# Score matmuls of a two-layer trunk: the keys' low parts in tiles of their own, zero on the other rows

## The chip, the cores and the metric

The kernel runs on one core of one Trainium2 chip. The metric is the device time of one execution in microseconds (us), the median over the runs; smaller is better. The engines are named as the profile names them: PE is TensorE's matmul, PEld its load of the stationary operand, DVE is VectorE, ACT is ScalarE, POOL is GpSimd, SP is SyncE, which here only issues DMAs.

## The reference

A trunk of two layers works on 256 latent tokens and 256 context tokens of width 1024. Each layer is a half-step SwiGLU FFN, a token mixer and a second half-step FFN, each behind an RMS norm that is modulated by a conditioning vector. Layer 0 mixes with differential attention (8 heads, two softmax maps of 64 features each), layer 1 with grouped-query attention (16 query heads, 4 key heads of 64 features, queries and keys normalised). Latent tokens attend to all 512 keys, context tokens to the 256 of the context.

```python
def _diff_attend(q, k, v, lam):
    s = jnp.einsum("bqhmd,bkhmd->bhmqk", q, k).astype(jnp.float32) * DA_HEAD_DIM ** -0.5
    p = jax.nn.softmax(s, axis=-1)
    p = (p[:, :, 0] - lam * p[:, :, 1]).astype(v.dtype)
    return jnp.einsum("bhqk,bkhe->bqhe", p, v)
...
def gqa_attend(q, k, v, scale):
    s = jnp.einsum("bqhgd,bkhd->bhgqk", q, k).astype(jnp.float32) * scale
    p = jax.nn.softmax(s, axis=-1).astype(v.dtype)
    return jnp.einsum("bhgqk,bkhd->bqhgd", p, v)
```

## The kernel before

Everything is held feature-major: 128 features on the partitions, tokens along the free dimension. An fp32 operand is split exactly into two float32r parts, hi and lo, and a product is the sum of three matmuls (`mac`, L383): hi with hi, hi with lo, lo with hi. Weights come in 512 KB pieces through SP's DMA queue, ACT makes the hi part (L152) and DVE the lo part (L153).

Scores need only 64 features, half of the 128 rows. So the kernel stacks the parts. `stack_q` (L606) puts the hi part of a map's or head's queries on its own 64 rows and the lo part on the other 64. `stack_k` (L616) puts the hi part of the keys on both halves. One matmul over all 128 rows (L626) then gives hi·hi and lo·hi together. The third term, the queries' hi part with the keys' lo part, is a second matmul over the 64 own rows alone (L627). Both maps of a head (m = 0, 1) share one tile `kl` for the lo parts: map 0 on rows 0 to 63, map 1 on rows 64 to 127. In the grouped-query layer two key heads share a `kl` in the same way.

Differential attention runs 8 heads of 4 units, a unit being 128 queries; units 0 and 1 (latent) see 512 keys, units 2 and 3 (context) 256. Each unit has two maps, so two pairs of score matmuls. After the scores come a DVE reduction (L733), the exponential on ACT (L734), DVE's normalisation and difference of the maps (L738 to L740), and one unit later PE's transposes (L750) and, once a head, the outputs (L761). Between the units stand products of the next head (`qk_proj`, `v_proj`) or of the output projection. The grouped-query layer runs 32 units of one pair each, 512 keys wide: reduction L1007, exponential L1009, normalisation L1011, transposes L1017 (up to two units later), outputs L1027 on 64 columns of the array, with query projections and pieces of the output projection between some units.

The order of instructions on each engine is set by the tile framework's scheduler, from the program's order and its own costs; the engines run their lists in order and wait on semaphores. Tiles are buffers of a pool; a tag with `bufs=n` has n of them, and a new tile waits until the old one's last reader is done.

At the head of differential attention, `lambdas` (L680) makes the scalar lambda from four vectors, `lamv`, that `late_constants` (L88) had loaded on SP's queue, and the context's norm is worked in among the first products: its sums of squares (`ms`, L272), 1/rms on ACT and DVE (L283 to L288, last `rsq`), its spread over the partitions on PE (`bc`, L315), and eight normalised tiles, each in a temporary `ht` (tag "ht", three buffers), as hi (L344) and lo (L345). The rotary embedding (`rotate`, L596) has one multiplication on POOL (L603). `sck` holds the conditioning vectors for the first norm's shift and scale. `pT` are the transposed weights of a unit (L751).

Of the kernel before, what the change touches and what calls it, by code (L numbers as in the profile page):

```python
# [19 lines left out]
P = 128  # L20
# [28 lines left out]
def trunk(ctx: ExitStack, tc: tile.TileContext, a: dict):  # L49
# [17 lines left out]
    tok = (slice(0, SEQ), slice(SEQ, T))  # L67
    sck = const.tile([P, KD, 32], F32, name="sck")
# [16 lines left out]
    lamv = const.tile([P, 4, 64], F32, name="lamv")  # L85
    rope = const.tile([P, 2, SEQ], F32, name="rope")

    def late_constants():  # L88
        nc.sync.dma_start(final_g, a["final_g"])
        nc.sync.dma_start(subln_g, a["da_subln_g"])  # L90
        nc.sync.dma_start(qk_g[:, 0:1], a["gqa_q_norm_g"])
        nc.sync.dma_start(qk_g[:, 1:2], a["gqa_k_norm_g"])
        for i, n in enumerate(("da_lam_q1", "da_lam_k1", "da_lam_q2", "da_lam_k2")):
            nc.sync.dma_start(lamv[:, i, :], a[n].to_broadcast([P, 64]))
        nc.sync.dma_start(rope, a["rope"])
# [17 lines left out]
    # a chunk is (its source, k tiles of each piece, columns of a k tile)  # L113
# [85 lines left out]
    def mod_first(pool, j):  # L199
        """Shift and scale of the first norm's feature tile j, on the tensor engine."""  # L200
# [26 lines left out]
    def first_rstd(pool, fp):  # L227
        """1 / rms of each token of both streams, on every partition."""
        ms = ax_tile("ms0")
        for j in range(0, KD, 2):  # L230
            sq = [fp.tile([P, T], F32, tag=t, name=f"sq_{t}") for t in ("sg", "av")]
            for i in range(2):
                nc.scalar.activation(sq[i], x[j + i], AF.Square)
            nc.vector.tensor_tensor(sq[0], sq[0], sq[1], op=ALU.add)
            for t in range(4):
                # one group for the whole bank
                nc.tensor.matmul(
                    ms[:, t : t + 1], sq[0][:, t * P : t * P + P], ones_d, start=(j, t) == (0, 0),
                    stop=(j, t) == (KD - 2, 3),
                )  # L240
# [12 lines left out]
    acc = [[stat.tile([P, 256], F32, name=f"sqacc{s}", tag=f"sqacc{s}"), None] for s in range(2)]  # L253

    def sq_add(j, s):
        if j == 0:
            nc.scalar.activation(acc[s][0], x[j][:, tok[s]], AF.Square)
        elif j == KD - 1:
            # the last feature tile's stay apart: the tensor engine adds them
# [7 lines left out]
    def mean_squares(s):  # L267
        ms = ax_tile("ms")
        for i in range(2):
            for t in range(2):  # L270
                # one group for the bank
# [6 lines left out]
    def rsqrt(pool, ms, n, scale=1.0, eng=nc.vector, tag="rsq"):  # L278
        """1 / sqrt(scale * ms + EPS), [P, n]: from the table's, made exact by a Newton step."""
# [11 lines left out]
    def rsqrt_free(pool, ms, n, scale=1.0, tag="rsq"):  # L291
        """1 / sqrt(scale * ms + EPS), [P, n], of positive values and without a table: from the halved
        exponent's bits, then a cubic and a Newton step."""
# [17 lines left out]
    def spread(r):  # L311
        """r, by tokens, on every partition."""
# [9 lines left out]
    def rms_rstd(s):  # L322
        """1 / rms of each token of a stream, on every partition."""
        return spread(rsqrt(tmp, mean_squares(s)[:, 0:2], 2))

    def table(func, after):
        """Has the activation table of func loaded once `after` is there."""
# [21 lines left out]
    def gained_shift(l, n3, j):  # L349
        """The shift as two more tokens, in parts."""  # L350
# [3 lines left out]
    def gained_tile(l, n3, j):  # L354
        """x times the norm's gain, without 1 / rms, which is a factor of each token."""
# [6 lines left out]
    # the context's norm, in steps that the next sublayer's first products are set between  # L362
# [20 lines left out]
    def mac(out, lhs, rhs, first, last):  # L383
        """out += lhs.T @ rhs, from the parts (hi, lo) of both."""
# [31 lines left out]
    def gained(j):  # L416
        """x times the final gain, by tokens."""
# [15 lines left out]
    def boundary(groups, nxt, follow):  # L433
        """The last products of a sublayer, first for the latent tokens, whose next norm then runs
        under the products for the context. A group is (outs, ends, tiles)."""
# [15 lines left out]
    def ffn(l, s, n, follow=None, f_steps=0, o_steps=0, upto=(0, 0)):  # L451
# [5 lines left out]
        with ExitStack() as st:  # L457
# [22 lines left out]
            def gated_late(i, gate, up):  # L480
                """Of products without 1 / rms, with those of the shift behind them."""
# [114 lines left out]
    def rotate(pool, t, tiles=1):  # L596
        """Axial rotary of t, [P, tiles * SEQ], in place."""
# [8 lines left out]
    def stack_q(q, st, scale):  # L606
        """Parts of -scale * the queries of two maps or heads (rows 0-63 and 64-127), each as one
        stack of hi and lo; hi stays on its own rows. scale is a power of two, or its negative."""
# [6 lines left out]

    def stack_k(k, st, lo):  # L616
        """Parts of the keys of two maps or heads: hi on both halves of the rows, lo on its own."""
        for m in range(2):
# [3 lines left out]
            nc.vector.tensor_tensor(lo[own], k[own], st[m][own].bitcast(F32), op=ALU.subtract)  # L622

    def scores(ps, q, k, k_lo, m):
        """ps = queries.T @ keys from the stacks of one map or head."""
        nc.tensor.matmul(ps, q, k, start=True, stop=False)  # L626
        nc.tensor.matmul(ps, q[HALF[m]], k_lo[HALF[m]], start=False, stop=True)  # L627
# [8 lines left out]
    def out_proj(base, parts, part, l, n, half, follow=None):  # L636
        """x += gate * (half of the heads) @ w_o; parts of these heads' outputs."""
# [34 lines left out]
    def diff_attention(l):  # L672
        base = start["att", l]
        scale = 64 ** -0.5
        with tc.tile_pool(name="da", bufs=2) as ap:
            lam = ap.tile([P, 4], F32, tag="lam", name="lam", bufs=1)
            nlam = lam[:, 3:4]
            g1 = ap.tile([P, 1], F32, tag="g1", name="g1", bufs=1)

# [22 lines left out]
            def stacks(qps, kps):  # L702
# [8 lines left out]
                kl = ap.tile([P, T], F32R, tag="kl", name="kl")  # L711
# [4 lines left out]
            # A unit is 128 queries of a head: of latent tokens (u = 0, 1) with all keys, of context  # L716
            # tokens (u = 2, 3) with the context's.
# [4 lines left out]
            def weights_of(hd, u):  # L722
                """Both maps' softmax and their difference."""
# [6 lines left out]
                for m in range(2):  # L730
                    sps = ax_tile("sps")
                    scores(sps[:, :nk], qs[m][:, tq], ks[m][:, k0:], kl[:, k0:], m)
# [12 lines left out]
            def turned(hd, u):  # L745
# [5 lines left out]
                pT = ap.tile([P, 4, P], F32, tag="pT", name="pT", bufs=4)  # L751
                nc.scalar.activation(pT[:, : nk // P, :].rearrange("p k q -> p (k q)"), tps[:, :nk], AF.Copy)
# [20 lines left out]
            def normed(hd):  # L773
                """1 / rms of the outputs of a pair of heads."""
# [10 lines left out]
            def parts_of(hd, hi, lo):  # L785
                """Feature-major, with the gain, in parts."""
# [11 lines left out]
            def behind(hd, u):  # L798
                """What follows a unit's weights, once the next unit's are under way."""
# [33 lines left out]
            def qk_proj(h, g):  # L833
# [4 lines left out]
                if g:  # L838
                    sts[h] = stacks(qks[h, 0], ps)
# [4 lines left out]
            def fillers(h):  # L844
                """Products between the units of head h, by unit."""
                if h == HEADS - 1:
                    # the norms' outputs are not needed from here on
# [26 lines left out]
            sts[0] = stacks(*qkps)  # L874
# [25 lines left out]
    def gqa(l):  # L900
        base = start["att", l]
        scale = 64 ** -0.5
        with tc.tile_pool(name="gq", bufs=2) as ap:
            qs = [ap.tile([P, SEQ], F32R, tag=f"qs{i % 8}", name=f"qs{i}", bufs=1) for i in range(16)]
            ks = [ap.tile([P, T], F32R, tag=f"ks{i}", name=f"ks{i}", bufs=1) for i in range(4)]
            kl = [ap.tile([P, T], F32R, tag=f"kl{i}", name=f"kl{i}", bufs=1) for i in range(2)]
# [8 lines left out]
            def rms_of(sq, tag, rsqrt):  # L915
                """1 / rms over the 64 features of each token of [P, 512]: by tokens, [P, 4 x 2 heads]."""
# [28 lines left out]
            def q_out(i, ps):  # L945
                sq = squares(ps)
                # the norm itself, a factor of each query, waits for the exponent
# [39 lines left out]
            for g in range(2):  # L987
                kn = k_normed(kps[g], kr[g])
                stack_k(kn, ks[2 * g : 2 * g + 2], kl[g])
# [5 lines left out]
            # A unit is 128 queries (qi) of one head (hb) of a tile t.  # L995
            def weights_of(t, qi, hb):
# [4 lines left out]
                scores(sps, qs[2 * t + hb][:, qi * P : qi * P + P], ks[2 * g + hb], kl[g], hb)  # L1001
# [180 lines left out]
```

## Time and profile before

| | |
|---|---|
| time, median of 3 runs | 1755.96 us (1752.56 to 1759.06) |
| profiled execution, first to last instruction (span; the profile leaves no other time of it) | 1750.3 us |
| PE busy | 1736.8 us, 99% of the span |
| PEld busy | 1469.2 us, 84% |
| DVE busy | 1162.5 us, 66% |
| ACT busy | 733.5 us, 42% |
| POOL busy | 22.1 us, 1% |
| granted TensorE clock, mean | 0.995 |
| differential attention's units | about 437 to 632 us of the span |
| grouped-query units | about 1448 to 1534 us of the span |

Matmuls are pipelined: a record's duration runs into those after it, so that the time that a matmul takes of the engine is read from its start to the next one's start, or from the chain of waits, which gives each piece the time that it adds. A PE that is busy is not PE at its peak. "issue" as the end of a wait means that the profile shows nothing that was waited for. Times below are from the span's start.

### The profile page before, as it was taken

To read this page: it belongs to the slowest core of one execution; us is meant where nothing else is said; L and a number is where in the kernel's file an instruction comes from. 1 tells how busy PE (TensorE), PEld (TensorE's weight loads), DVE (VectorE), ACT (ScalarE), POOL (GpSimd) and SP (SyncE) were. 2 spreads that over 40 slices of the span, in tenths; PEclk is the share of its full clock that TensorE was granted. 3 is DMA by queue.
4 is the path that set the end of the run, shared out by engine and by line. 5 is a ranking of instruction groups with operands and counts; after the bars stand their busy time and mean duration, and the time that the engine had idled before them with its cause. 6 is when DMAs were issued, how large, how long until landed. Compare 5 with 4: busy or idle time off the path is not lost.

```text
span 1750.3 us, 24875 instructions
## 1 busy us (share of the span) xinstructions
PE 1736.8 (99%) x9586; PEld 1469.2 (84%) x9586; DVE 1162.5 (66%) x2113; ACT 733.5 (42%) x1359; POOL 22.1 (1%) x34
## 2 busy tenths in 40 slices
PE   9999999999999999999999999999999999999998
PEld 6788888889778789888888898888888897699998
DVE  3697786757777778765866557545452498776664
ACT  3432222235656656222222244322232377765454
POOL 0000000000000000000000000000000000000000
PEclk8999999999999999999999999999999999999999
DMA  7675655442112122545644535446552331145652
GB/s 258 226 237 166 191 204 185 151 138 87 59 49 73 60 86 85 200 135 158 203 151 165 155 111 190 151 125 197 177 162 79 109 121 49 49 151 154 215 155 87
DMA packets 76870, 249.58 MB, mean 143 GB/s; under 512 B 9937, under 2 KB 10065, under 8 KB 76753
## 3 DMA queue, kind: packets, MB, share of 16 engines
q1 hardware_dynamic: 76032, 247.38, 43.7%
q8 instruction: 75, 1.23, 0.3%
q10 hardware_dynamic: 720, 0.62, 0.1%
q14 instruction: 43, 0.34, 0.1%
HBM read 246.92 MB, written 1.05 MB: 142 GB/s over the span
## 4 chain that ended last, share of the span: by engine, by line
PE 98%; DVE 1%; ACT 0%; issue 0%; POOL 0%; DVEq 0%; ACTq 0%
PE out L387 7%; PE out L388 7%; PE out L386 7%; PE gate L386 7%; PE gate L388 7%; PE up L388 7%; PE gate L387 7%; PE up L386 7%; PE up L387 7%; PE sps L627 2%; PE qk L386 2%; PE g L386 2%; PE qk L388 2%; PE qk L387 2%; PE sps L626 2%; PE g L387 2%
## 5 line engine op out<-in xcount | busy, mean ns | idle before, releaser
L152 ACT ACTIVATE whi<-raw 128x1024 fp32r<-128x1024 f32 (+3 forms) x426 | 350.9, 836 | 485.3 <-PE out L387 253.2
L153 DVE TENSOR_TENSOR wlo<-raw,whi 128x1024 fp32r<-128x1024 f32 (+3 forms) x426 | 399.6, 946 | 194.5 <-ACT whi L152 193.8
L174 DVE CUSTOM_DVE_ANT_0 junk<-wm,sc,b_mod 128x1024 bf16<-128x1024 f32 x224 | 287.4, 1283 | 179.0 <-DMA wm<-in_w_mod 175.1
L386 PE MATMUL gate<-hhi,whi 128*128 128x512 f32 (+1 forms) x648 | 233.8, 361 | 0.0
L388 PE MATMUL gate<-hhi,wlo 128*128 128x512 f32 (+1 forms) x648 | 233.8, 361 | 0.0
L387 PE MATMUL up<-hlo,whi 128*128 128x512 f32 (+1 forms) x648 | 233.7, 361 | 0.0
L387 PE MATMUL gate<-hlo,whi 128*128 128x512 f32 (+1 forms) x648 | 233.7, 361 | 0.0
L386 PE MATMUL up<-hhi,whi 128*128 128x512 f32 (+1 forms) x648 | 233.7, 361 | 0.0
L388 PE MATMUL up<-hhi,wlo 128*128 128x512 f32 (+1 forms) x648 | 233.7, 361 | 0.0
L387 PE MATMUL out<-alo,whi 128*128 128x512 f32 (+1 forms) x638 | 232.6, 365 | 0.0
L388 PE MATMUL out<-ahi,wlo 128*128 128x512 f32 (+1 forms) x638 | 232.2, 364 | 0.0
L386 PE MATMUL out<-ahi,whi 128*128 128x512 f32 (+1 forms) x638 | 232.1, 364 | 0.0
L387 PEld LDWEIGHTS out<-alo,whi 128*128 128x128 f32 x638 | 119.9, 188 | 21.5 <-DVE alo L405 0.4
L386 PEld LDWEIGHTS gate<-hhi,whi 128*128 128x128 f32 x648 | 122.3, 189 | 18.5 <-ACT sg L474 0.2
L387 PEld LDWEIGHTS up<-hlo,whi 128*128 128x128 f32 x648 | 122.3, 189 | 18.4
L388 PEld LDWEIGHTS gate<-hhi,wlo 128*128 128x128 f32 x648 | 122.3, 189 | 18.4
L388 PEld LDWEIGHTS up<-hhi,wlo 128*128 128x128 f32 x648 | 122.3, 189 | 18.3
L386 PEld LDWEIGHTS up<-hhi,whi 128*128 128x128 f32 x648 | 122.3, 189 | 18.3
L387 PEld LDWEIGHTS gate<-hlo,whi 128*128 128x128 f32 x648 | 122.3, 189 | 18.3
L386 PEld LDWEIGHTS out<-ahi,whi 128*128 128x128 f32 x638 | 120.0, 188 | 20.9
L388 PEld LDWEIGHTS out<-ahi,wlo 128*128 128x128 f32 x638 | 119.9, 188 | 21.0
L404 ACT ACTIVATE ahi<-av 128x512 fp32r<-128x512 f32 (+1 forms) x88 | 50.8, 578 | 181.3 <-DVE av L476 174.1
(239 smaller groups left out, 2630.8 us busy)
## 6 DMA issues: line engine op xcount, KB each, us to landing
raw<-in_w_in SPq DMA_DIRECT2D x170, 512.0 KB, 4.5
wm<-in_w_mod SPq DMA_DIRECT2D x128, 512.0 KB, 4.2
raw<-in_w_out SPq DMA_DIRECT2D x64, 384.0 KB, 3.2
raw<-in_w_out SPq DMA_DIRECT2D x64, 320.0 KB, 3.1
raw<-in_da_vqk SPq DMA_DIRECT2D x24, 512.0 KB, 3.6
wf<-in_w_mod SPq DMA_DIRECT2D x16, 512.0 KB, 4.7
raw<-in_gq_qkv SPq DMA_DIRECT2D x12, 512.0 KB, 3.7
raw<-in_da_o SPq DMA_DIRECT2D x8, 512.0 KB, 3.6
```

Source lines behind the costliest of these rows:

```text
L152: nc.scalar.activation(hi[:, c], raw[:, c], AF.Copy)
L153: nc.vector.tensor_tensor(lo[:, c], raw[:, c], hi[:, c].bitcast(F32), op=ALU.subtract)
L174: nc.vector.tensor_tensor_reduce(out=junk, in0=raw, in1=mod_pool["sc"][:, s, :], op0=ALU.mult, op1=ALU.add, scale=1.0, scalar=b_mod[:, l, ...
L386: nc.tensor.matmul(out, ah, bh, start=first, stop=False)
L387: nc.tensor.matmul(out, ah, bl, start=False, stop=False)
L388: return nc.tensor.matmul(out, al, bh, start=False, stop=last)
L404: nc.scalar.activation(hi, src, AF.Copy)
L626: nc.tensor.matmul(ps, q, k, start=True, stop=False)
L627: nc.tensor.matmul(ps, q[HALF[m]], k_lo[HALF[m]], start=False, stop=True)
```

## The change

Each map or key head gets a `kl` tile of its own, [128, 512]; the lo part stays on its own 64 rows, and the other 64 rows are set to zero once, by POOL, at the start of each attention (`zero_others`, 8 memsets in all). The second score matmul then goes over all 128 rows with the same stationary queries as the first: the zero rows add nothing. In differential attention the four `kl` tiles are made once (two per head, taken in turn by even and odd heads).

The added tiles take space, and four tiles move for it. `lamv` is loaded by ACT's DMA queue at the start of differential attention into an `ht` buffer, no longer by SP among the late constants; `sck` lies in a temporary; `pT` has two buffers of 512 and two of 256 columns, before four of 512.

```diff
+    sck = tmp.tile([P, KD, 32], F32, tag="sq", name="sck")
...
-        for i, n in enumerate(("da_lam_q1", "da_lam_k1", "da_lam_q2", "da_lam_k2")):
-            nc.sync.dma_start(lamv[:, i, :], a[n].to_broadcast([P, 64]))
...
+    def zero_others(lo):
+
+        for m in range(2):
+            nc.gpsimd.memset(lo[m][HALF[1 - m]].bitcast(F32), 0.0)
...
-            nc.vector.tensor_tensor(lo[own], k[own], st[m][own].bitcast(F32), op=ALU.subtract)
+            nc.vector.tensor_tensor(lo[m][own], k[own], st[m][own].bitcast(F32), op=ALU.subtract)
...
-        nc.tensor.matmul(ps, q[HALF[m]], k_lo[HALF[m]], start=False, stop=True)
+        nc.tensor.matmul(ps, q, k_lo, start=False, stop=True)
...
+            lamv = tmp.tile([P, 4, 64], F32, tag="ht", name="lamv")
+            for i, n in enumerate(("da_lam_q1", "da_lam_k1", "da_lam_q2", "da_lam_k2")):
+                nc.scalar.dma_start(lamv[:, i, :], a[n].to_broadcast([P, 64]))
+
+            kls = [[ap.tile([P, T], F32R, tag=f"kl{i}{m}", name=f"kl{i}{m}", bufs=1) for m in range(2)] for i in range(2)]
+            for kl in kls:
+                zero_others(kl)
...
-                kl = ap.tile([P, T], F32R, tag="kl", name="kl")
+                kl = kls[h % 2]
...
-                    scores(sps[:, :nk], qs[m][:, tq], ks[m][:, k0:], kl[:, k0:], m)
+                    scores(sps[:, :nk], qs[m][:, tq], ks[m][:, k0:], kl[m][:, k0:])
...
-                pT = ap.tile([P, 4, P], F32, tag="pT", name="pT", bufs=4)
+                pT = ap.tile([P, nk // P, P], F32, tag=f"pT{nk}", name="pT")
...
-            kl = [ap.tile([P, T], F32R, tag=f"kl{i}", name=f"kl{i}", bufs=1) for i in range(2)]
+            kl = [ap.tile([P, T], F32R, tag=f"kl{i}", name=f"kl{i}", bufs=1) for i in range(4)]
+            for g in range(2):
+                zero_others(kl[2 * g : 2 * g + 2])
...
-                scores(sps, qs[2 * t + hb][:, qi * P : qi * P + P], ks[2 * g + hb], kl[g], hb)
+                scores(sps, qs[2 * t + hb][:, qi * P : qi * P + P], ks[2 * g + hb], kl[2 * g + hb])
```

On PE one thing moves. At the head of differential attention the spread of the context's 1/rms (`bc`) stands, before, right behind the last product for the values (`v`) and ahead of the first for queries and keys (`qk`):

```order
L388 MATMUL v_3281<-whi_1_3236,hlo_141 128x256
L315 MATMUL bc<-ident,rsq 128x128 x2
L386 MATMUL qk_3282<-hhi_126,whi_0_3251 128x256
L387 MATMUL qk_3282<-hlo_134,whi_0_3251 128x256
L388 MATMUL qk_3282<-hhi_126,wlo_0_3252 128x256
```

Now twelve of the `qk` matmuls stand ahead of it; these are the last ones before it and the first behind it, with the changed kernel's line numbers (two less):

```order
L386 MATMUL qk_3290<-hhi_127,wlo_0_3247 128x256
L384 MATMUL qk_3290<-hhi_128,whi_0_3246 128x256
L385 MATMUL qk_3290<-hlo_136,whi_0_3246 128x256
L386 MATMUL qk_3290<-hhi_128,wlo_0_3247 128x256
L313 MATMUL bc<-ident,rsq 128x128 x2
L384 MATMUL qk_3291<-hhi_125,whi_0_3246 128x256
```

The score matmuls stand where they stood. On DVE, at the same place, lambda's two products (`lj`, `lam`) read `lamv` between the steps of the context's 1/rms (`rsu`, `rsq`). Before, with the data there since the opening:

```order
L285 TENSOR_TENSOR rsu<-rsm,rsq 128x2
L683 ISA lj,lam<-lamv 128x64
L683 ISA lam 128x1
L286 TENSOR_TENSOR rsu<-rsu,rsq 128x2
L691 TENSOR_SCALAR g_3271<-subln_g 128x1
L683 ISA lj,lam<-lamv 128x64
L683 ISA lam 128x1
L287 TENSOR_SCALAR rsu<-rsu 128x2
```

Now, with `lamv` on its way from ACT's queue, where its four DMAs stand right behind the last square of the context's norm (`sq`); the second product stands behind `rsq` and ahead of the first normalised tile (`ht`):

```order
L283 TENSOR_TENSOR rsu<-rsm,rsq 128x2
L151 TENSOR_TENSOR wlo_1_3620<-raw_1_3617,whi_1_3619 128x512
L284 TENSOR_TENSOR rsu<-rsu,rsq 128x2
L695 ISA lj,lam<-lamv 128x64
L695 ISA lam 128x1
L285 TENSOR_SCALAR rsu<-rsu 128x2
L151 TENSOR_TENSOR wlo_1_3620<-raw_1_3617,whi_1_3619 128x512
L286 TENSOR_TENSOR rsq<-rsu,rsq 128x2
L695 ISA lj,lam<-lamv 128x64
L695 ISA lam 128x1
L701 TENSOR_TENSOR lam<-lam 128x1
L702 TENSOR_SCALAR lam<-lam 128x1
```

So the step of the context's norm that PE's `bc` waits for is now queued on DVE behind a DMA that is issued some microseconds earlier.

## Rows read from the trace of the kernel before

**Rows 1.** The page: the span, the busy time of the engines, and the shares of the chain that ended last.

```profile
span 1750.3 us, 24875 instructions
...
PE 1736.8 (99%) x9586; PEld 1469.2 (84%) x9586; DVE 1162.5 (66%) x2113; ACT 733.5 (42%) x1359; POOL 22.1 (1%) x34
...
PE 98%; DVE 1%; ACT 0%; issue 0%; POOL 0%; DVEq 0%; ACTq 0%
```

**Rows 2.** Groups of instructions by line and shape, PE: line, engine, operation, tiles, rows*columns of the array, shape, count, then busy us, mean ns of one, idle before. `sps` are the scores.

```profile
L627 PE MATMUL sps<-kl,qs 64*128 64x512 f32 x64 | 31.8, 496 | 0.0
L626 PE MATMUL sps<-ks,qs 128*128 128x512 f32 x64 | 30.6, 478 | 1.9 <-ACT ks L621 1.8
...
L627 PE MATMUL sps<-kl,qs 64*128 64x256 f32 x32 | 12.2, 380 | 0.0
L626 PE MATMUL sps<-ks,qs 128*128 128x256 f32 x32 | 11.8, 370 | 0.0
```

**Rows 3.** The chain of waits at the first units of differential attention, in order of time: start us, us that the piece adds, what. All pieces are 512 columns wide.

```profile
438.64 0.23 PE qk L386
438.87 0.23 PE sps L626
439.11 0.43 PE sps L627
439.54 0.43 PE sps L626
...
440.82 0.42 PE sps L627
441.25 0.44 PE qk L387
441.68 0.23 PE qk L388
```

**Rows 4.** The timeline of the loads at the same place: start us, duration us, what; in brackets the idle time of the load path before it and what ended it.

```profile
438.48 0.19 PEld L626 LDWEIGHTS sps<-ks,qs 128*128 128x128 f32 x1
439.03 0.18 PEld L627 LDWEIGHTS sps<-kl,qs 64*128 64x128 f32 x1 [0.36 <-issue]
439.46 0.19 PEld L626 LDWEIGHTS sps<-ks,qs 128*128 128x128 f32 x1 [0.25 <-issue]
```

**Rows 5.** The chain of waits at a context unit, 256 columns wide.

```profile
474.83 0.12 PE sps L626
474.95 0.31 PE sps L627
...
475.88 0.32 PE v L386
476.20 0.12 PE v L387
```

**Rows 6.** The chain's shares by line, first in 440 to 632 us (differential attention's units), then in 1448 to 1534 us (grouped-query units).

```profile
by line: PE qk L386 13.4%; PE qk L388 12.5%; PE qk L387 12.4%; PE sps L627 11.8%; PE ops L761 9.8%; PE sps L626 8.5%; PE v L386 6.5%; PE v L387 6.1%; PE v L388 6.0%; PE tps L750 5.9%; PE op L386 2.0%; PE op L388 1.9%; PE op L387 1.8%; PE ot
...
by line: PE ops L1027 19.6%; PE tps L1017 18.9%; PE sps L627 14.9%; PE sps L626 11.7%; PE q L386 5.1%; PE op L386 5.1%; PE q L387 4.9%; PE q L388 4.4%; PE op L388 4.3%; PE op L387 4.3%; PE nms L919 2.3%; ACT pe L1009 0.9%; DVE mx L1007 0.8%
```

**Rows 7.** The chain of waits among the grouped-query units: two groups of four transposes (`tps`), the first behind a product, the second behind a second score matmul, then a place where DVE ends a wait.

```profile
1458.35 0.44 PE tps L1017 x4
...
1461.12 0.59 PE tps L1017 x4
...
1468.60 0.69 DVE mx L1007
```

**Rows 8.** Busy time by stretch: from:to us, length, then busy us of PE, PEld, DVE, ACT, POOL (instructions), granted clock, DMA share, GB/s. The first is differential attention's units, the others are the grouped-query units in four parts.

```profile
437.00:632.00 195.00, 194.94 (x1058) 155.25 (x1059) 151.98 (x341) 125.20 (x328) 11.00 (x14) 1.00 0.17 57
1448.00:1473.00 25.00, 24.59 (x139) 15.84 (x137) 21.97 (x60) 20.52 (x45) 0.74 (x1) 1.00 0.21 72
1473.00:1497.00 24.00, 24.00 (x164) 17.74 (x164) 20.74 (x61) 18.09 (x41) 3.06 (x2) 1.00 0.11 37
1497.00:1511.00 14.00, 13.03 (x77) 9.04 (x76) 11.34 (x41) 9.53 (x21) 0.00 (x0) 1.00 0.11 38
1511.00:1534.00 23.00, 22.98 (x150) 16.65 (x149) 15.35 (x42) 16.37 (x35) 0.00 (x0) 1.00 0.15 47
```

**Rows 9.** Differential attention, a unit's weights done on DVE (timeline, DVE) and its transposes on PE (chain of waits).

```profile
490.76 0.75 DVE L740 SCALAR_TENSOR_TENSOR pe<-pe,ls 128x512 f32<-128x512 f32 x1
...
501.86 0.44 PE tps L750 x4
```

**Rows 10.** The head of differential attention and `lamv`: the timeline of ACT, DVE and PE there, then lines of the view of `lamv`, whose DMAs are on SP's queue.

```profile
407.86 0.40 ACT L261 ACTIVATE sq<-x 128x256 f32<-128x256 f32 x1
...
411.29 0.15 DVE L288 TENSOR_TENSOR rsq<-rsu,rsq 128x2 f32<-128x2 f32 x1
...
411.73 0.61 PE L315 MATMUL bc<-ident,rsq 128*128 128x128 f32 x4
...
L94 SPq DMA_DIRECT2D lamv<-in_da_lam_q x2: 430/430/430, 65.1 to 66.0; - x2
...
DMA to landing us min/median/max: 4.5/5.6/6.5
```

**Rows 11.** POOL: a memset of the opening (groups by line), and the first rotation of differential attention (timeline).

```profile
L69 POOL MEMSET sck<- 128x256 f32 x1 | 0.3, 311 | 0.3 <-POOLq L1171 0.3
...
430.45 0.97 POOL L603 TENSOR_TENSOR qk<-qk,rope 128x256 f32<-128x256 f32 x1 [428.60 <-DVE sw L601]
```

More of the change, by code (lines that the diff above doesn't have):

```diff
@@ L67, in trunk @@
     tok = (slice(0, SEQ), slice(SEQ, T))
-    sck = const.tile([P, KD, 32], F32, name="sck")
+    sck = tmp.tile([P, KD, 32], F32, tag="sq", name="sck")
     nc.gpsimd.memset(sck, 0.0)
@@ L84, in trunk @@
     qk_g = const.tile([P, 2], F32, name="qk_g")
-    lamv = const.tile([P, 4, 64], F32, name="lamv")
     rope = const.tile([P, 2, SEQ], F32, name="rope")
@@ L621, in stack_k, with scores @@
             nc.scalar.activation(st[m][other], k[own], AF.Copy)
-            nc.vector.tensor_tensor(lo[own], k[own], st[m][own].bitcast(F32), op=ALU.subtract)
-    def scores(ps, q, k, k_lo, m):
+            nc.vector.tensor_tensor(lo[m][own], k[own], st[m][own].bitcast(F32), op=ALU.subtract)
+    def scores(ps, q, k, k_lo):
         nc.tensor.matmul(ps, q, k, start=True, stop=False)
-        nc.tensor.matmul(ps, q[HALF[m]], k_lo[HALF[m]], start=False, stop=True)
+        nc.tensor.matmul(ps, q, k_lo, start=False, stop=True)
     def out_piece(w, parts, part, l, n, jq, i):
@@ L700, in v_out, with stacks @@
                 nc.scalar.activation(v[:, t::2, :], ps.rearrange("p (s f) -> p s f", s=2), AF.Copy)
-            def stacks(qps, kps):
+            def stacks(h, qps, kps):
                 f32 = []
@@ L750, in turned @@
                     nc.tensor.transpose(tps[:, kt * P : kt * P + P], pe[:, 0, kt * P : kt * P + P], ident)
-                pT = ap.tile([P, 4, P], F32, tag="pT", name="pT", bufs=4)
-                nc.scalar.activation(pT[:, : nk // P, :].rearrange("p k q -> p (k q)"), tps[:, :nk], AF.Copy)
+                pT = ap.tile([P, nk // P, P], F32, tag=f"pT{nk}", name="pT")
+                nc.scalar.activation(pT.rearrange("p k q -> p (k q)"), tps[:, :nk], AF.Copy)
                 hd["pT"].append(pT)
@@ L838, in qk_proj @@
                 if g:
-                    sts[h] = stacks(qks[h, 0], ps)
+                    sts[h] = stacks(h, qks[h, 0], ps)
             def o_piece(f):
@@ L873, in diff_attention @@
                 v_out(vs[0], t, vps[t])
-            sts[0] = stacks(*qkps)
+            sts[0] = stacks(0, *qkps)
             prev = None
@@ L988, in gqa @@
                 kn = k_normed(kps[g], kr[g])
-                stack_k(kn, ks[2 * g : 2 * g + 2], kl[g])
+                stack_k(kn, ks[2 * g : 2 * g + 2], kl[2 * g : 2 * g + 2])
                 if g == 0:
```

## The prediction

> **What bounds the kernel now.** I read the page first: PE is busy 1736.8 of 1750.3 us and the chain that ended last lies on PE for 98% [rows 1]. So an edit counts if it shortens PE's own sequence, or if it makes PE wait. Then I looked for PE time that is not streaming. The groups by shape show two score matmuls per map or head: 64 pairs that are 512 columns wide and 32 that are 256 wide, the first on 128 rows, the second on 64 [rows 2]. Their mean durations overlap with their neighbours, so their price comes from the chain of waits. There a whole-array product adds 0.23 us for 512 columns, and so does a first score matmul behind a product (438.87). The second score matmul adds 0.43 (439.11), the whole-array score behind it 0.43 as well (439.54), and so does a product behind one (441.25: 0.44, its successor 0.23 again) [rows 3]. At 256 columns it is 0.31 for 0.12, and 0.32 for the product behind it [rows 5]. The loads tell why: the load for 438.87 starts at 438.48, while an earlier matmul still streams; the load on 64 rows at 439.03 and the whole-array load behind it at 439.46 start only after 0.36 and 0.25 us of idle load path [rows 4]. Each change between 128 and 64 rows leaves one load uncovered, some 0.2 us, and each pair has two such changes.
>
> **The second matmul on 128 rows.** Number and order of the score matmuls stay; only the rows change. I take the price of a 128-row matmul behind another for both: 0.23 (512) and 0.12 (256).
>
> In differential attention the chain from 440 to 632 us gives L627 11.8% and L626 8.5% of 192 us, 39.0 us [rows 6]. Some 62 pairs lie there (two and a half of 64 before 440), 32 of 256 columns and 30 of 512: without uncovered loads 2 x (32 x 0.12 + 30 x 0.23) = 21.5. That saves 17.5, and the early pairs about 1.0. Behind a second score matmul stand also 26 products, each 0.20 cheaper (0.43 to 0.23, or 0.32 to 0.12): 5.2; and 8 groups of transposes, 0.15 each (0.59 behind a second score matmul, 0.44 behind a product [rows 7]): 1.2. I counted these followers in the records of PE. Together 24.9 us.
>
> In the grouped-query units, 1448 to 1534, L627 has 14.9% and L626 11.7% of 86 us, 22.9 [rows 6]; 32 pairs x 2 x 0.23 are 14.7; that saves 8.2. Behind the second one stand 7 products (1.4) and 14 groups of transposes (2.1). Together 11.7. The few scores next to the outputs on 64 columns keep an uncovered load; I leave that within the rounding.
>
> The ceiling is 36.6 us, if PE alone decides. Below, the cost of the matmul itself is bounded by the row that stands nearest: a whole-array score between two switches is 0.43, as the 64-row one, so the edit cannot cost more than nothing there.
>
> **What is late next.** In differential attention DVE is busy 151.98 of 195 us and ACT 125.20 [rows 8]; with 24.9 us less, DVE fills 89%. It has time in hand: a unit's weights were ready at 491.51 and PE turned them only at 501.86 [rows 9]. I expect nearly all of it, less about 1 us in the first and last units, where no products stand between.
>
> The grouped-query units are tighter. In 1448 to 1473 DVE is busy 21.97 of 25 us and ACT 20.52; in 1473 to 1497 DVE 20.74 of 24; in 1497 to 1511 PE itself already idles about 1 us, and only 1511 to 1534 is loose, DVE 15.35 of 23 [rows 8]. At one place the chain already goes through DVE's reduction (1468.60) [rows 7]. Sharing the 11.7 by length: the first stretch could save 3.4 but would then be shorter than DVE's work, so I take 1.5; the second 2.5 of 3.3; the third 1.0 of 1.9; the last all of 3.1. That is 8.1, a loss of 3.6. The ends are 0 (DVE holds it all) and 11.7.
>
> **The head of differential attention.** `lamv` now comes by four DMAs behind ACT's last square, which ends at 408.26 [rows 10]. An issue took 0.43 us on SP and a landing 4.5 to 6.5 us, so the first two vectors are there between about 413.2 and 415.6, the last by 416.5. DVE waits for them ahead of `rsq`, which ended at 411.44 before; behind it wait PE's `bc` and the eight tiles. PE's `bc` stands twelve matmuls later, 12 x 0.12 = 1.4 us behind 411.73. So PE could wait there up to some 4 us; or not at all, if ACT's emptier queue lands them sooner. I take 1.5, with 0 and 4 as ends.
>
> **Edits at nothing.** The memsets: 128x256 took 0.31 us on POOL [rows 11]; a 64x512 one I bound by half and twice that, so four take at most 2.5 us. The first rotation, the next in POOL's queue, comes at 430.45, some 25 us behind the last FFN products; without that cover those 2.5 us would be the cost. DVE's subtractions into `kl` keep their number and size. The `kl` tiles alternate by head, as the two buffers did; `pT` has two buffers for each width, and a head writes two of each, as before. SP loses four issues (1.7 us) at 65 us, where PE is covered; `sck` moves in space alone.
>
> **Sum.** 24.9 - 1.0 + 8.1 - 1.5 = 30.5. I say 30: 1750.3 becomes about 1720 in the span. The median stands 5.7 us above the profiled span; I leave that as it is: 1756 - 30 = 1726 us.
>
> **Rivals.** (1) The other engines hold both attentions. For it: the four tight places above. Against it: the 10 us in hand in differential attention. If the grouped-query units gave nothing, the head took 4 and differential attention gave half, the saving would be 8 to 20 us: 1736 to 1748.
>
> (2) It does not do what it says: a load on the same rows cannot run under a matmul, so the second pair member stays at 0.43 whether its rows are 64 or 128. Against it are the products' loads, whole-array behind whole-array, which add 0.23 and have their load under way 0.39 us ahead (438.48 for 438.87) [rows 3, 4]. L386 and L387 of such a product even load the same stationary operand twice in a row, as the new pair will. For it is only that no score pair of that form stands in the trace. Saving 0, less 1.5 at the head: 1757. The Trainium skill ("TensorE: Matmul & The Clock Gate", section "The mechanism") says just this: a load overlaps with matmuls in flight only when its row group differs. By that sentence the 128-row form would give nothing; the trace disagrees with it for products, and I go by the trace.
>
> (3) Slower: `lamv` lands so late that DVE, and behind it PE, stand still at the head of the attention. Cover is the 3.0 us from the square's end at 408.26 to `rsq` at 411.29 and the 1.4 us of moved matmuls; every microsecond beyond these 4.4 costs one. To eat the 30 and end 0.5% above 1756 the landing would have to take some 43 us (4.4 + 30 + 8.8), against 4.5 to 6.5 in the row; at 45 us the time would be 1726 + 40.6 = 1767.
>
> **Chances.** Forecast, with most of the pairs' loads hidden: 0.87, 1718 to 1736. Rival 1: 0.08, of which about 0.01 ends within 0.5%. Rival 2: 0.03. Rival 3 and unforeseen losses: 0.02. 0.5%, 8.8 us, is about what a measurement of this kernel can tell from no change. So faster 0.94, within 0.5% 0.04, slower 0.02. The range: the ceiling of 36.6 gives 1719.4, with a microsecond or two for the measurement 1718; the lower ends of the unknown costs (head 4, grouped-query 0) leave 24.9 - 1.0 - 4 = 19.9, 1736, and I go to 1738 to take in a part of rival 1.
>
> **What would show it.** Right: in the chain of waits both score matmuls at 0.23 (or 0.12) and products behind them at the usual price; their loads at 128x128 and under way before the matmul; differential attention's units some 24 us shorter; more waits of PE for DVE or ACT in the grouped-query units, which shrink by about 8. A wait of `bc` for `rsq`, behind `lamv`'s DMA, would show the head's cost. Wrong, if the second score matmul still adds 0.43 (rival 2), if the attentions' length stays while PE waits for DVE (rival 1), or if the time is lost outside the attentions, where nothing moves.

## The result, and the profile after

The changed kernel takes 1730.42 us (median of 4 runs, 1729.97 to 1731.05) beside 1754.26 of the kernel before in the same comparison (4 runs, 1751.72 to 1759.06): ratio 0.9859, 95% interval [0.9845, 0.9874]. The profiled span falls from 1750.3 to 1727.8 us, by 22.5. Forecast were 1726 us, from a saving of 30.

The page of the changed kernel: span, busy time, and the shares of the chain that ended last.

```profile
span 1727.8 us, 24899 instructions
...
PE 1707.0 (99%) x9586; PEld 1463.1 (85%) x9586; DVE 1159.4 (67%) x2113; ACT 730.3 (42%) x1359; POOL 26.3 (2%) x42
...
PE 84%; DVE 7%; issue 3%; DMA 2%; ACT 2%; POOL 0%; DVEq 0%; ACTq 0%; POOLq 0%
```

PE has the same 9586 matmuls and 29.8 us less busy time, but the chain that was PE's for 98% [rows 1] is now PE's for 84%. The groups by shape of the score matmuls, all on 128 rows now (lines 630 and 631 were 626 and 627):

```profile
L630 PE MATMUL sps<-ks,qs 128*128 128x512 f32 x64 | 28.9, 452 | 3.3 <-ACT ks L625 3.1 <-ACT pe L1023 0.2
L631 PE MATMUL sps<-kl,qs 128*128 128x512 f32 x64 | 25.7, 402 | 0.0
...
L630 PE MATMUL sps<-ks,qs 128*128 128x256 f32 x32 | 9.7, 323 | 0.0
L631 PE MATMUL sps<-kl,qs 128*128 128x256 f32 x32 | 8.3, 281 | 0.0
```

The chain of waits at places like those of [rows 3] and [rows 5], and the loads as in [rows 4]:

```profile
441.46 0.23 PE sps L631
441.70 0.23 PE sps L630
441.93 0.23 PE sps L631
...
442.61 0.23 PE qk L385
...
446.72 0.12 PE sps L630
446.84 0.13 PE sps L631
```

```profile
441.31 0.19 PEld L630 LDWEIGHTS sps<-ks,qs 128*128 128x128 f32 x1
441.54 0.19 PEld L631 LDWEIGHTS sps<-kl,qs 128*128 128x128 f32 x1
441.77 0.19 PEld L630 LDWEIGHTS sps<-ks,qs 128*128 128x128 f32 x1
```

Each score matmul, and the product behind the pair, adds 0.23 us (0.12 at 256 columns) where it added 0.43 (0.31). The loads follow every 0.23 us, with no idle time in brackets. What came instead stands in the list of what PE waited for (us in total, times, longest):

```profile
PE sps L630 <- ACT ks L625: 3.1, 2, 1.8
PE ops L773 <- ACT pT L764: 1.4, 3, 0.6
...
PE tps L762 <- DVE pe L752: 0.8, 1, 0.8
PE gate L384 <- DVE av L474: 0.7, 1, 0.7
PE bc L313 <- DVE rsq L286: 0.7, 1, 0.7
```

Of these, only 1.8 us of the first stood in the trace before, as the second line of [rows 2] shows. The stretches of [rows 8], at nearly the same work:

```profile
437.00:614.00 177.00, 171.37 (x1052) 149.88 (x1051) 150.44 (x340) 123.00 (x322) 11.07 (x14) 1.00 0.19 63
1432.00:1455.00 23.00, 21.59 (x141) 15.72 (x137) 21.24 (x58) 20.18 (x44) 0.73 (x1) 1.00 0.22 71
1455.00:1478.00 23.00, 23.00 (x167) 17.86 (x166) 21.32 (x63) 18.75 (x43) 3.05 (x2) 1.00 0.14 46
1478.00:1491.00 13.00, 11.47 (x77) 8.82 (x76) 11.49 (x41) 9.42 (x22) 0.00 (x0) 1.00 0.14 41
1491.00:1512.00 21.00, 20.95 (x149) 16.34 (x148) 14.84 (x42) 16.13 (x35) 0.00 (x0) 1.00 0.16 51
```

Where the 22.5 us came from is read from the starts of the same matmul in two traces, which works here because every kernel below has the same 9586. The marks are matmuls that begin at 403.89, 430.83, 649.89, 1433.13 and 1539.85 us in the kernel before. In the table stands by how much each stretch is longer (+) or shorter in one profiled execution:

| kernel | opening and first FFN, to 404 | head of the differential attention, to 431 | differential attention, to 650 | three FFN parts, to 1433 | grouped-query, to 1540 | rest | span |
|---|---|---|---|---|---|---|---|
| changed | +1.62 | +0.98 | -18.37 | +0.01 | -6.30 | -0.43 | 1727.8 |
| moves_only | +0.28 | +0.80 | +0.01 | -0.01 | -0.01 | -0.76 | 1750.6 |
| gqa_only | +2.51 | -0.01 | +2.95 | +0.01 | -6.31 | -0.82 | 1748.6 |
| grouped64 | -0.54 | -0.01 | -14.11 | +0.05 | +0.06 | -0.81 | 1735.0 |
| lam_early | +2.49 | +0.05 | -18.38 | -0.01 | -6.26 | +0.33 | 1728.5 |
| relieved_before | +2.93 | 0.00 | +5.89 | +0.01 | +6.79 | -0.37 | 1765.6 |
| relieved_after | +1.23 | +0.88 | -19.95 | +0.01 | -6.23 | -0.30 | 1726.0 |
| act_before | -0.18 | -0.01 | 0.00 | +0.01 | -0.73 | -0.33 | 1749.1 |
| act_after | -0.07 | +0.96 | -21.14 | +0.05 | -5.17 | +0.60 | 1725.6 |
| outputs_late | +1.61 | +1.11 | -16.43 | +0.01 | -6.33 | -0.38 | 1729.9 |
| best1 | -0.72 | +0.06 | -16.11 | -0.04 | -6.25 | -0.48 | 1726.8 |
| best2 | +3.37 | +0.05 | -18.35 | -0.11 | -1.86 | -0.75 | 1732.7 |
| deep | -0.90 | +0.06 | -18.39 | -0.05 | -6.41 | +0.09 | 1724.7 |

The stage columns repeat to about 0.1 us wherever the code of a stage is the same and the clock stayed up (-18.37, -18.38, -18.39); the first column does not, whatever the code. So the stages are compared by this table, and the whole by the runs.

### The profile page after: what moved, and what is told of

It is laid out like the page before. It is cut to its first block, busy times and chain, and to the rows that moved or that the text cites. A ratio compares the mean times of both kernels' runs of the same rounds, so it can differ in the third digit from the quotient of the medians.

```text
span 1727.8 us, 24899 instructions
## 1 busy us (share of the span) xinstructions
PE 1707.0 (99%) x9586; PEld 1463.1 (85%) x9586; DVE 1159.4 (67%) x2113; ACT 730.3 (42%) x1359; POOL 26.3 (2%) x42
## 3 DMA queue, kind: packets, MB, share of 16 engines
q8 instruction: 75, 1.23, 0.3%
## 4 chain that ended last, share of the span: by engine, by line
PE 84%; DVE 7%; issue 3%; DMA 2%; ACT 2%; POOL 0%; DVEq 0%; ACTq 0%; POOLq 0%
PE out L385 7%; PE out L386 7%; PE out L384 7%; PE gate L384 7%; PE gate L385 7%; PE gate L386 7%; PE up L385 7%; PE up L386 7%; PE up L384 7%; DMA wm<-in_w_mod 2%; PE g L384 2%; PE g L385 2%; PE g L386 2%; DVE junk L172 1%; PE e L384 1%
## 5 line engine op out<-in xcount | busy, mean ns | idle before, releaser
L386 PEld LDWEIGHTS gate<-hhi,wlo 128*128 128x128 f32 x648 | 122.4, 189 | 18.4
L385 PEld LDWEIGHTS up<-hlo,whi 128*128 128x128 f32 x648 | 122.4, 189 | 18.4
L384 PEld LDWEIGHTS up<-hhi,whi 128*128 128x128 f32 x648 | 122.4, 189 | 18.4
L386 PEld LDWEIGHTS out<-ahi,wlo 128*128 128x128 f32 x638 | 119.7, 188 | 21.1
```

Of the source, the lines that this page charges most:

```text
L384: nc.tensor.matmul(out, ah, bh, start=first, stop=False)
L385: nc.tensor.matmul(out, ah, bl, start=False, stop=False)
L386: return nc.tensor.matmul(out, al, bh, start=False, stop=last)
```

## The experiments

**The change apart: its moves, and one attention alone.** `moves_only` keeps the 64-row scores and takes the rest of the change; `gqa_only` has full rows in the second attention alone.

```diff
-        for i, n in enumerate(("da_lam_q1", ...)):
-            nc.sync.dma_start(lamv[:, i, :], ...)
+            lamv = tmp.tile([P, 4, 64], F32, tag="ht", name="lamv")
+                nc.scalar.dma_start(lamv[:, i, :], ...)
```

> The kernel before with the change's moves alone: lambda's vectors loaded by ACT at the head of the differential attention, sck in a scratch tile, two pT rings; the score matmuls stay as they were. Theory M (the moves cost about 2.6 us of the shortfall): slower than before by about 2.6 us, of which some 1.3 to 1.6 in the opening, before 330 us of the span, and 1.0 at the head of the attention near 415 us; the attentions themselves unchanged. Rival N (the moves are free and the 2.6 us belong to the profiled execution alone): 0, within 0.5 us, in both places.

> The kernel before with full rows in the grouped-query attention alone (and sck in a scratch tile, for the room). Theory T (the two attentions add up, each by its own uncovered loads less its own new waits): the span falls by 6 to 7 us, all of it between 1430 and 1535 us, and the differential attention stays as before. Rival U (the grouped-query part gains only because the differential attention ahead of it changed, or the reverse): under 4 or over 9 us.

`moves_only`: 1755.55 us, ratio 1.0007 [0.9997, 1.0018]. The head costs 0.80 us, as Theory M has it. The opening does not: +0.28, while `gqa_only` and `relieved_before`, whose `lamv` was not moved, have +2.51 and +2.93 there. Of these, 1.0 and 1.5 us arise in the first 75 us, and 1.5 in each at one place of the first FFN, where DVE waits for a weight (`wm`) and PE's `gate` then waits for DVE's `av`. That DVE instruction began at 305.48 us in the kernel before and at 309.21 in `gqa_only`, as their timelines show (the first is of before):

```profile
305.48 1.28 DVE L174 CUSTOM_DVE_ANT_0 junk<-wm,sc,b_mod 128x1024 bf16<-128x1024 f32 x1 [3.46 <-DMA wm<-in_w_mod]
```

```profile
309.21 1.28 DVE L174 CUSTOM_DVE_ANT_0 junk<-wm,sc,b_mod 128x1024 bf16<-128x1024 f32 x1 [3.45 <-DMA wm<-in_w_mod]
```

The DMA lands earlier or later by execution, with or without the move. For the opening Theory M falls.

`gqa_only`: 1748.01 us, ratio 0.9964 [0.9950, 0.9978], and -6.31 us in its stage against -6.30 in the changed kernel. Theory T holds: the attentions add up. (Its +2.95 in the differential attention, whose code is that of before, is told last.)

**Is it the switch or the 64-row matmul?** `grouped64` is the kernel before in another order:

```diff
-                    scores(sps[:, :nk], qs[m][:, tq], ks[m][:, k0:], kl[:, k0:], m)
+                for m in range(2):
+                    nc.tensor.matmul(sp[m][:, :nk], qs[m][:, tq], ks[m][:, k0:], start=True, stop=False)
+                for m in range(2):
+                    nc.tensor.matmul(sp[m][:, :nk], qs[m][HALF[m], tq], kl[HALF[m], k0:], start=False, stop=True)
```

> The kernel before, where the differential attention issues the full-row score matmuls of both maps first and then the two 64-row ones of the unit next to each other; nothing is zero-padded and the number of matmuls stays. Theory S (what cost time was each change between 128 and 64 rows, about 0.2 us each, four in a unit): two changes fewer in each of 32 units, so some 0.4 us a unit, 8 to 13 us in all less a few us of new waits of the first map's softmax, and the second full load and the second 64-row load are covered (0.23 us spacing between the two full ones at 512 columns). Rival D (a 64-row matmul is dear by itself, whatever stands beside it): 0, within 2 us, each 64-row matmul still 0.43 us. Rival P (two 64-row matmuls on different halves of the rows run side by side): more than 13 us, the pair taking less than 0.3 us together.

1741.52 us, ratio 0.9923 [0.9908, 0.9938]; -14.11 us in the stage. The chain of waits there, in order of time (x2 stands for two instructions), then the timeline of PE at the same place:

```profile
438.99 0.67 PE sps L732 x2
439.65 0.43 PE sps L734 x2
440.09 0.43 PE qk L387
440.51 0.23 PE qk L388
```

```profile
439.58 0.51 PE L734 MATMUL sps<-kl,qs 64*128 64x512 f32 x2
```

The two full matmuls add 0.67, as 0.43 and 0.23 would: only the one behind the switch has an uncovered load. The two 64-row ones add 0.43 together, begin at the same time and are both done within 0.51 us. Rival D is out, and Theory S's price holds: a switch costs 0.2 us. But the gain lies above its 8 to 13 us. Rival P's running side by side is there too, on top of it, in gain (more than 13) though not in its price under 0.3 us, as the pair's own load is uncovered. The padded form still gains more, 18.37, since two switches of each unit remain here.

**Lambda's loads.** `lam_early` is the changed kernel with the loads on SP again, ahead of `rope`, and lambda's two products in the opening.

> The changed kernel with lambda's vectors loaded by SP with the other late constants again, into a scratch tile, and their two products taken by DVE in the opening; full-row scores in both attentions as changed. Theory M (lambda's move costs 1.0 us at the attention's head and 1.3 to 1.6 in the opening): faster than the changed kernel by 1.0 to 2.6 us, the wait of the matmul bc for DVE's rsq near 415 us gone. Rival N (that wait is replaced by the next, the matmul's chain over sq and rsq alone): 0, within 0.5 us.

1728.07 us, ratio to before 0.9850 [0.9835, 0.9865]. The wait of `bc` is gone and the head costs 0.05 instead of 0.98, as in `best1`, `best2` and `deep`. The whole is not told apart from the changed kernel, as the intervals overlap.

**What PE waits for in the attentions.** Two pairs of kernels leave DVE's normalisation out; the second pair also moves a copy.

```diff
-                nc.vector.reciprocal(ls, ls)
-                nc.vector.tensor_scalar(pe, pe, ls, None, op0=ALU.mult)
...
-                nc.scalar.activation(dst, src, AF.Copy)
+                nc.vector.tensor_copy(dst, src)
```

> The kernel before without the softmax's normalisation in either attention: DVE's reciprocal of the row sums, its scaling of the weights and, in the differential attention, the difference of the two maps are left out; every matmul, transpose and ACT instruction stays. It is the partner of the same cut in the changed kernel. Theory W (the missing part of the gain is TensorE waiting for DVE and ACT in the attentions, which it hardly did before): this kernel is within 3 us of the kernel before, since TensorE was bound there by its own loads. Rival C (the ceiling of 36.6 us was too high): the same here.

> The changed kernel with the same DVE instructions left out. Against its partner, over the two attentions alone (span's starts at about 430 and 637, 1432 and 1535 us), Theory W: the gain grows from 24.7 us (18.4 and 6.3) to 32 to 36 us (23 to 25 and 9 to 11.5), as the waits go with DVE's work. Rival C (fewer loads were uncovered than counted, and the waits in the trace only replace others): it stays at 23 to 27 us.

> The kernel before without the softmax's normalisation in either attention, and with the copy of the turned weights out of PSUM (pT) in the grouped-query attention made by DVE instead of ACT: DVE has there about what it had (0.69 us more, 0.63 less a unit), ACT 0.6 us less a unit. It is the partner of the same cut in the changed kernel; what counts is the grouped-query stage, from 1432 us of the span to the last FFN. Theory A (ACT's chain, the exponential and the copy, is what the changed kernel waits for there): the stage is within 2 us of the kernel before, since its own loads bound it. Rival L (the order of the stage bounds both): the same.

> The changed kernel with the same cut and the same move. Theory A: the grouped-query stage, 77 us in the changed kernel, is 2 to 5 us shorter than there, so that the gain of the stage over its partner goes from 6.3 to 8.5 to 11.5 us, and most first score matmuls of a unit run at 0.23 us instead of 0.32 to 0.34. Rival L (one head's chain from score over exponential, turn and output, and PSUM's banks, bounds the stage, whichever engine has less to do): within 1 us of the changed kernel.

`relieved_before` took 1760.78 us, ratio 1.0034 [1.0017, 1.0051]: with less work on DVE it was slower. In its profiled execution PE's clock fell (below), so it is no partner for a stage; its two runs with a granted clock of 0.995 took 1754.1 and 1754.7 us. `act_before` (1756.26; 1.0011 [0.9998, 1.0024]) kept its clock, has the same code in the differential attention, and is as long there as the kernel before (0.00).

In the differential attention the changed form gains 21.1 us with DVE relieved (`act_after`, 1727.41; 0.9848 [0.9828, 0.9867]) instead of 18.4. Taking the distance from each matmul to the next one by one, and leaving out changes under 0.02 us, those that grew add up to 6.1 us in the changed kernel and to 2.8 here; those that shrank to 24.3 and 24.1. So some 3.3 us of the new waits were DVE's normalisation, and the rest is ACT's, as the waits of `act_after` in this attention show (the first 1.8 us as before):

```profile
PE sps L630 <- ACT ks L625: 2.2, 2, 1.8
PE ops L768 <- ACT pT L759: 1.2, 3, 0.4
```

Theory W is half right here, below its 23 (`relieved_after`, with the same code there, shows 19.95, with a fall of the clock). In the grouped-query units it fails: beside the kernel before, -6.23 (`relieved_after`, 1726.23; 0.9843 [0.9829, 0.9857]) and -5.17 (`act_after`), no more than -6.30; beside its partner `act_before`, whose stage is 0.73 shorter, `act_after` gains 4.4. That is below Theory A's 8.5 to 11.5 as well, but the test is not clean: the moved copies now stand in the chain of waits themselves, which in `act_after` has, among others,

```profile
1444.67 0.60 DVE pT L1027
1445.27 0.60 DVE mx L1016
1445.87 0.60 DVE pT L1027
```

Why there was so little to win is told under the prediction's steps.

**Outputs a unit later.**

```diff
-U_AT = 0
+U_AT = 1
...
-                    outputs(hd)
...
+                        owed.append(hd)
```

`U_AT` moves the transposes of the outputs (`otps`) a unit later as well.

> The changed kernel, where the differential attention issues a head's outputs one unit later, beside the next head's first unit, so that their ACT copy of pT has time. Theory W: the waits of the matmuls ops for ACT's pT (1.9 us in three places) and of otps for DVE's o (0.6 in two) go, 1.5 to 2.5 us in all between 480 and 585 us. Rival Q (ACT is as late one unit later, because it is behind by its whole queue): 0, within 0.5 us, the same wait at another matmul.

1731.87 us, ratio 0.9875 [0.9859, 0.9891]. The stage gains 16.43 instead of 18.37: neither theory. The waits of `ops` for ACT are gone from the list, and others are there, between 480 and 560 us:

```profile
PE otps L803 <- DVE o L795: 3.2, 2, 1.6
PE tps L762 <- DVE pe L752: 0.7, 2, 0.3
```

**Versions that might be better.** `best1` joins early lambda and late outputs; `best2` is `lam_early` with some high parts copied by POOL (`nc.gpsimd.tensor_copy`); `deep` is `lam_early` with three grouped-query units in flight (`n >= 3` for `n >= 2`).

> Lambda's early loads and the late outputs together, on the changed kernel. Theory W with M: 1.0 us from the head of the differential attention and 1.5 to 2.5 from the outputs, 2.5 to 3.5 us below the changed kernel. Rival Q with N: 0 to 1 us.

> The changed kernel with lambda's early loads, and with the high parts of the grouped-query attention's later weights (12 us of copies) made by POOL instead of ACT. Theory A: ACT has 0.3 us a unit less to do and the stage is 0.5 to 2 us shorter; with lambda's 1.0 us about 2 us below the changed kernel. Rival L: the stage as long as before, only lambda's 1.0 us. Rival B (POOL is slow at this, and DVE waits for its high parts or loses time beside it): the stage 0.5 us or more longer.

> The changed kernel with lambda's early loads, where the grouped-query attention has three units in flight instead of two: a unit's transposes, and what follows them, are issued one unit later behind its scores (the pieces of the output product move along). Theory L (what the changed kernel lost there is the length of one unit's chain, score, exponential, scaling, transpose, with too few units beside it): the grouped-query stage, 6.3 us shorter in the changed kernel than before, is another 2 to 5 us shorter, with less of the stage's chain of waits on DVE and ACT. Rival E (the work of DVE and ACT as a whole, and the key and query preparation at the stage's head, holds it): within 1 us of the changed kernel, or longer by up to 2 us, because the last units then stand closer together at the end.

`best1`: 1730.16 us, 0.9865 [0.9850, 0.9880], the head gained and the outputs lost. `best2`: 1733.54, 0.9882 [0.9863, 0.9900]; its grouped-query stage gains 1.86 instead of 6.3, with DVE waiting 2.0 us for POOL's parts: Rival B. `deep`: 1729.76, 0.9866 [0.9846, 0.9886]; -6.41, so Rival E. None is told apart from the changed kernel.

## Why the prediction held, and where its sum was off

**The mechanism: right.** The loads of a 128-row pair are under way ahead of their matmuls, the chain shows 0.23 and 0.12, and `grouped64` shows that the switch is what cost. (The lead of 0.39 us in the prediction is measured to 438.87, where the chain lets the piece begin; the matmul's own record starts at 438.71, 0.23 behind its load.) Rival 2 is out. The Trainium skill ("TensorE: Matmul & The Clock Gate", section "The mechanism") has a sentence that a load overlaps only with matmuls of another row group; with this the trace does not agree, as loads of 0.19 us start every 0.23 us under whole-array matmuls, with no idle time before them. The same section also lets a load go ahead when it goes to a background buffer; no run here tells where these loads go.

**Differential attention: the ceiling was right, "nearly all of it, less about 1 us" was not.** The distances that shrank add up to 24.3 us, forecast 24.9. But 6.1 us came back as waits in single places: 1.5 us in the last head for ACT's `ks`, 1.0 in the last unit of the first head for DVE's `pe`, 0.6 to 0.7 three times for ACT's `pT`, 0.3 twice at `otps`. The step that failed read the slack from one unit that had 10 us in hand [rows 9] and from DVE's mean of 89%. In the trace before, the 32 units had 0.3 to 10.6 us in hand, and the one that now costs 1.0 us had 0.95. DVE was in fact busy 150.44 of 177 us, 85%. ACT, at which the larger part of these waits ends and by which the prediction did not judge, was busy 123.00, 69%. A mean and one slack unit do not speak for the units that have little in hand.

**Grouped-query units: 6.3 for 8.1, and the step that failed is the ceiling of 11.7.** The distances that shrank add up to 8.65 us, those that grew to 2.35. In the four stretches of [rows 8] it gained 2.1, 1.4, 0.9 and 1.9 us, where 1.5, 2.5, 1.0 and 3.1 were forecast. In the last one no distance grew, and seven pairs gave 1.9 us, 0.27 each; 0.27 x 32 is 8.6. The prediction had 11.7 / 32 = 0.37 for every pair (with 14 groups of transposes behind pairs, where the records have 13). Three of the seven gave 0.33 to 0.36, near that price. The one between outputs on 64 columns, which I had left "within the rounding", gave 0.19: there the second score matmul followed the first by 0.44 us before and by 0.34 after, not by 0.23. The other three gave 0.2 each. Two of them were held by a wait that PE's list does not show, as PE counts as busy (20.95 of 21 us) while the record of an earlier matmul runs. It stands in the timeline of the loads, in brackets (0.23 and 0.24 before):

```profile
1501.10 0.19 PEld L630 LDWEIGHTS sps<-ks,qs 128*128 128x128 f32 x1 [0.23 <-ACT pe L1023]
1501.86 0.19 PEld L630 LDWEIGHTS sps<-ks,qs 128*128 128x128 f32 x1 [0.46 <-ACT pe L1023]
```

Such a load waits for ACT's exponential of an earlier unit, the last reader of one of the three buffers that scores and products share (`mm_ps`). The list of what the loads of the first score matmuls waited for has it (us in total, times, longest), before and in the changed kernel:

```profile
PEld sps L626 <- ACT pe L1009: 1.2, 4, 0.4
```

```profile
PEld sps L630 <- ACT pe L1023: 3.3, 10, 0.6
```

So part of what the padding covered came back as a wait for ACT, and the split into 8.65 and 2.35 does not separate the two. The prediction took its 3.6 off for DVE's busy time. Neither relieved kernel shortens the exponential: there the loads still wait for it, 2.4 us (`relieved_after`) and 2.2 (`act_after`) in 4 places each, and the transposes (`tps`) wait for it too, 2.7 and 3.1, which fits that they won nothing. A kernel with more buffers for the scores was not tried, so how much of the 3.3 us can be won stays open.

**The head: 1.5 forecast, 0.8 to 1.0 measured.** The step was right, DVE waiting for `lamv` ahead of `rsq` and `bc` waiting for `rsq` (0.7 in the list). DVE's timeline, then lines of the view of `lamv`:

```profile
414.63 0.23 DVE L695 CUSTOM_DVE_ANT_0 lj<-lamv 128x64 f32<-128x64 f32 x1 [1.52 <-DMA lamv<-in_da_lam_k]
```

```profile
L686 ACTq DMA_DIRECT2D lamv<-in_da_lam_q x2: 334/394/453, 409.2 to 410.1; - x2
...
DMA to landing us min/median/max: 3.4/4.8/5.4
```

They landed a little sooner than the 4.5 to 6.5 us of [rows 10].

**Edits at nothing: right.** The four memsets took 2.24 us, within the bound, at a time when POOL had nothing else:

```profile
407.06 2.24 POOL L617 MEMSET kl<- 64x512 f32 x4 [405.21 <-PE e L386]
```

**The sum.** 24.3 - 6.1 and 8.65 - 2.35 less 1.0 at the head make 23.5; the rest is the 1.6 us of the opening, 1.3 of them behind a late `wm`, and 0.4 to the other side. That the time came closer (1726 for 1730.42) than the saving (30 for 22.5 in the span) is luck. I carried 5.7 us from span to median unchanged, and the median of the changed kernel lies only 2.6 us above its profiled span. Every run of it lies 2.1 to 2.2 us above its own span, and so does every run of the kernel before whose span is known; by the same 2.2 the other 3.5 us of the 5.7 were a median run that was longer than the profiled one. Rival 3 had the right place, but cost 1.0 of the 39 us that it needed.

## What to carry to other kernels

Where a load path waits again and again between matmuls of different row counts, padding the smaller with zeros was worth more here than the rows it wastes, as the matmul itself cost no more (0.23 us for 0.43); where that is no option, setting the small ones next to each other on different halves gets most of it (14.1 of 18.4 us here). Count the gain per place from what stands before and behind each matmul, not from the price between products. And when the bounding engine gets a tenth faster in a stage, look for the single units where the others are late, since DVE at a mean of 85% busy and ACT at 69% already cost a quarter of the gain, and read the waits of the loads beside those of the matmuls.

## What had not been expected

**The clock.** In `gqa_only` the differential attention is the code of the kernel before, and yet 3 us longer. By windows: from:to us, length, busy us of PE, PEld, DVE, ACT, POOL, granted clock, DMA share, GB/s.

```profile
438.00:440.00 2.00, 0.44 (x2) 0.21 (x2) 1.41 (x3) 1.73 (x3) 0.00 (x0) 1.00 0.09 18
440.00:442.00 2.00, 2.00 (x7) 1.12 (x6) 1.74 (x4) 1.63 (x4) 0.00 (x0) 0.82 0.63 238
442.00:444.00 2.00, 2.00 (x4) 0.72 (x3) 0.81 (x3) 1.17 (x4) 0.72 (x1) 0.50 0.02 6
...
446.00:448.00 2.00, 2.00 (x6) 1.55 (x5) 2.00 (x7) 0.78 (x2) 0.00 (x0) 0.50 0.00 0
448.00:450.00 2.00, 2.00 (x10) 1.63 (x9) 0.85 (x3) 1.46 (x3) 0.00 (x0) 0.97 0.00 0
```

PE had waited 1.8 us for `ks`, as in the kernel before, then the granted clock fell from 1.00 (2.4 GHz) to 0.50 (1.2 GHz) for some 7 us. In `relieved_before` it fell at the same place and twice in the grouped-query stage, which fits its +5.89 and +6.79. In the changed kernel's profile the same wait left it at 1.00, but in `relieved_after` it was 0.79 from 437 to 445, so full rows do not rule it out. The kernel before spread over 1751.66 to 1757.50 us in one comparison of 17 runs, the changed one over 1.1 in 4. The mean granted clock of each run shows that the clock goes with this spread: of 54 runs of the kernel before, the 29 at 0.995 or 0.996 took 1751.3 to 1753.6 us, the 17 at 0.992 or 0.993 took 1756.2 to 1758.6. The first group's median is 1752.2, so of the 23.8 us between the medians of the two kernels (1754.26 and 1730.42) some 2 go with the clock; beside that group the change gains about 22, as in the span. Of the kernels with 64-row matmuls in the differential attention, 45 of 100 runs show 0.993 or less; of those with full rows there, none of 32 but the one of the next paragraph. That uncovered loads favour the falls fits this but was not shown: the kernels differ in other ways too.

**A record that costs nothing.** In the profiled execution of `act_after` the clock column reads 0.95 wherever the others read 1.00. The three FFN parts took as long as before (+0.05), so that reading alone is no loss.
